# A block's high part meets both parts of x in one product of 512 columns; a tile's two sums share a PSUM bank

## The chip, the cores and the metric

The kernel runs on one core of a Trainium2 chip. Its time is the device time of one launch in microseconds, median of three runs. TensorE (PE) multiplies, with its weight loads shown as an engine of their own (PEld); VectorE (DVE) and ScalarE (ACT) do the elementwise work and read PSUM; GpSimd (POOL) and SyncE (SP) mostly issue DMAs.

## The reference, cut to what matters

x has 256 tokens of 2048 channels, in float32. Three residual parts follow one another, each with large projections of x:

```
x = x + lru_mlstm_layer(rmsnorm(x, e_norm), ...)   # u = x @ w_in; RG-LRU and mLSTM; y @ w_out
x = x + ssd_layer(rmsnorm(x, o_norm), ...)         # u = x @ w_in; SSD scan; y @ w_out
x = rmsnorm(x, final_norm)
h = rmsnorm_2(x, norm_mix)                         # one projection into S5, GLA, differential attention and gates
x = x + merged(h) @ w_out
x = x + ffn(...)                                   # up, convolution, gated silu, down
out = rmsnorm(x, norm_final)
```

Nearly all the arithmetic is in the products of x (or of an activation) with weight matrices of some 2048 x 8000; they must be near float32's accuracy.

## The kernel before

Channels lie on the partitions, the 256 tokens in the free dimension. Every weight matrix is cut on the host into blocks of 128x128, laid out in the order in which PE takes them: one stream of 8048 blocks in chunks of 8 (512 KB). `ahead` (L248) issues a chunk's DMA on SP up to three chunks early, and splits four blocks at a time, up to five such parts ahead: ACT copies them to a rounded float32r tile `wh` (L242), DVE subtracts it from the original and leaves the rest in `wl` (L243). Each has six buffers, given back as PE is through with them.

Activations are split in the same way into a tile of high parts and one of low parts, each [128, 2, 256]: two tiles of channels side by side (`split`, `split_into`; in `finish` with the next norm's weight). `kx` picks the tile of channels k from the pair.

`prod` (L269) multiplies one block: `h` with x's high part, `h` with its low part, `l` with its high part, three matmuls of 256 columns that add up in one PSUM region (L273, L274, L275). `mm` runs it over the KT blocks of each of two output tiles; the group fills one bank [128, 2, 256] from a pool `pm` of four banks. `mm_late` does the same for an output projection, whose first two pairs are begun before the last row tiles are ready, so that two groups are open at once. The other four banks (`ps`) serve the side work. The first layer opens three groups at once while x arrives (`begun`).

What reads a group is one instruction as a rule: DVE multiplies it with the row of 1/rms into a temporary tile (L559, L571, L626, L836, L907, L1030, L1056, L1573), or adds it to the residual (L474, L654); q, k, v and o are copied by ACT (L591 to L598, groups of 4 blocks per tile); in glu ACT takes the tanh of the second tile and DVE multiplies the first with it (L1082, L1083); for the other branches ACT doubles the group (L1101).

RG-LRU, mLSTM, SSD, S5, GLA and attention are generators; `pump`, called at the end of each `mm`, steps them, so their instructions stand between the groups. The framework takes the whole program, plans every engine's order by priorities in a simulated timeline in which buffers are given out in turn, and writes the waits. So the order on DVE and ACT is a planned one, fixed before the launch, and each of them takes its instructions strictly in that order.

Of the kernel before, what the change touches and what calls it, by code (L numbers as in the profile page):

```python
# [80 lines left out]
# per-channel parameters, as columns of 128 channels: name -> number of columns  # L81
# [15 lines left out]
# shape-only constants: name -> columns  # L97
# [17 lines left out]
def _constants():  # L115
# [6 lines left out]
    for r in range(8):  # L122
        c[r::32, COFF["sel8"] + r] = 1.0  # the sum over the four rows r, 32 + r, 64 + r, 96 + r
# [8 lines left out]
    for h in range(4):  # L132
        # rows q, columns k; the first half is the key tile before q's, the second q's own
# [16 lines left out]
class Builder:  # L150
    def __init__(self, nc, tc, d, dbg, ctx):
# [12 lines left out]
        # weight stream  # L164
# [9 lines left out]
        self.w_pos = 0  # blocks taken  # L174
        self.raw, self.hl = {}, {}

# [12 lines left out]
    def act(self, shape=(P, 2, T), dt=F32, pool=None):  # L189
        """storage of the present stage"""  # L190
# [19 lines left out]
    def psm(self, shape=(P, 2, T)):  # L210
        return self.pm.tile(list(shape), F32, name=self.nm("pm"), tag="pm", bufs=4)
# [14 lines left out]
    def _dma_chunk(self, i):  # L226
        """the first chunk comes in halves"""
# [20 lines left out]
    def ahead(self, part):  # L248
        """loads and splits that the blocks from this part on will need"""
# [19 lines left out]
    def prod(self, o, k, KT, xh, xl):  # L269
# [7 lines left out]
    def mm_late(self, KT, k0, np, xh, xl):  # L277
        """the first pairs of output tiles, in the order that late() gives -> PSUM tiles [128, 2, 256]"""
        p = [self.psm() for _ in range(np)]
        for n, k in late(2 * np, KT, k0, np):  # L280
            self.prod(p[n // 2][:, n % 2, :], k, KT, xh, xl)
# [6 lines left out]
    def mm(self, nt, KT, xh, xl):  # L288
        """nt (1 or 2) output tiles of KT blocks each -> PSUM tile [128, nt, 256]"""
        p = self.psm((P, nt, T))  # L290
        for n in range(nt):
            for k in range(KT):
                self.prod(p[:, n, :], k, KT, xh, xl)
# [18 lines left out]
    def drain(self, gen=None):  # L312
        """run the side work (or one piece of it) to its end"""
# [7 lines left out]
    def split_into(self, h, l, v, scale=None):  # L321
        """h, l: parts of v (times a power of two) that one pass carries each"""
# [29 lines left out]
    def colsum(self, tiles, add=True):  # L352
        """sum over the partitions (and over the tiles) -> PSUM [128 tokens, 2]"""
# [12 lines left out]
    def bcast(self, cols):  # L366
        """cols: [128 tokens, 2] -> PSUM [128, 256], row by row the same"""
# [23 lines left out]
    def log1pexp(self, u, w, n):  # L391
        """u = exp(-|x|) in (0, 1] -> log1p(u), as 2 atanh(u / (2 + u)); w: scratch of u's shape"""
# [12 lines left out]
    def conv(self, u, ws, b, taps, dst):  # L405
        """causal convolution along the tokens of one [128, 256] tile"""
# [6 lines left out]
    def exp_exact(self, x, n):  # L413
        """exp of a [128, n] tile to float32's accuracy"""
# [1318 lines left out]
```

## Time and profile before

| | |
|---|---|
| median of 3 runs | 3123.27 us (3122.21 to 3123.41) |
| profiled execution, span | 3120.4 us |
| PE busy, products | 99%, 26310 |
| weight loads busy | 98%, 26310 |
| DVE busy | 74%, 4693 instructions |
| ACT busy | 56%, 3303 instructions |
| DMA | 178 GB/s mean, 55.2% of 16 engines in the weights' queue |

The span runs from the first to the last instruction of the profiled execution; the page gives no other time of it. An engine's share says how long it had something running. The chain of waits goes back from the last instruction to what released it. In the rows, a name such as pm<-x,wh says that an instruction writes tile pm from x and wh; a row of a timeline begins with its start and duration in us, and may merge several instructions of a kind (xN); in brackets stands how long the engine was idle before it, and what ended that.

### The profile page before, as it was taken

To read this page: it belongs to the slowest core of one execution; us is meant where nothing else is said; L and a number is where in the kernel's file an instruction comes from. 1 tells how busy PE (TensorE), PEld (TensorE's weight loads), DVE (VectorE), ACT (ScalarE), POOL (GpSimd) and SP (SyncE) were. 2 spreads that over 40 slices of the span, in tenths; PEclk is the share of its full clock that TensorE was granted. 3 is DMA by queue.
4 is the path that set the end of the run, shared out by engine and by line. 5 is a ranking of instruction groups with operands and counts; after the bars stand their busy time and mean duration, and the time that the engine had idled before them with its cause. 6 is when DMAs were issued, how large, how long until landed. Compare 5 with 4: busy or idle time off the path is not lost.

```text
span 3120.4 us, 66894 instructions
## 1 busy us (share of the span) xinstructions
PE 3097.5 (99%) x26310; PEld 3048.5 (98%) x26310; DVE 2300.0 (74%) x4693; ACT 1748.8 (56%) x3303; POOL 90.9 (3%) x123
## 2 busy tenths in 40 slices
PE   8999999999999999999999999999999999999998
PEld 8999999999999999999999998999999999999998
DVE  8777766669888876778888786666677776567764
ACT  6666544556666555554555554555555555455554
POOL 1000000010000000120000000000000000000000
PEclk9999999999999999999999999999999999999999
DMA  7555555556555555665454554556556555655564
GB/s 236 178 182 161 176 160 183 183 181 213 183 189 175 166 179 179 193 203 173 152 155 149 164 169 149 163 162 199 185 183 184 183 183 184 188 183 184 183 187 151
DMA packets 153933, 556.30 MB, mean 178 GB/s; under 512 B 17392, under 2 KB 18544, under 8 KB 152592
## 3 DMA queue, kind: packets, MB, share of 16 engines
q1 hardware_dynamic: 148752, 534.89, 55.2%
q0 software_dynamic: 3104, 14.75, 1.3%
q8 instruction: 206, 3.38, 0.4%
q10 hardware_dynamic: 1760, 2.38, 0.2%
q14 instruction: 111, 0.91, 0.1%
HBM read 547.69 MB, written 4.26 MB: 177 GB/s over the span
## 4 chain that ended last, share of the span: by engine, by line
PE 99%; DVE 1%; ACT 0%; DMA 0%; issue 0%; SPq 0%; DVEq 0%
PE pm L273 31%; PE pm L275 31%; PE pm L274 31%; PE ps L997 1%; PE ps L1299 0%; PE ps L1337 0%; PE ps L1458 0%; PE ps L362 0%; PE ps L1284 0%; PE ps L1229 0%; PE ps L791 0%; PE ps L966 0%; PE ps L676 0%; PE ps L675 0%; PE ps L1433 0%; DMA w<-w_first 0%
## 5 line engine op out<-in xcount | busy, mean ns | idle before, releaser
L242 ACT CAST wh<-w 128x512 fp32r<-128x512 f32 (+1 forms) x2013 | 1239.3, 621 | 1233.6 <-PE pm L274 1080.1
L243 DVE TENSOR_TENSOR wl<-w,wh 128x512 fp32r<-128x512 f32 (+1 forms) x2013 | 1390.0, 696 | 652.2 <-ACT wh L242 630.4
L273 PE MATMUL pm<-x,wh 128*128 128x256 f32 x5504 | 1566.1, 285 | 5.9 <-ACT wh L242 5.9
L275 PE MATMUL pm<-x,wl 128*128 128x256 f32 x5504 | 1560.1, 284 | 3.1 <-DVE q L419 3.1
L274 PE MATMUL pm<-x,wh 128*128 128x256 f32 x5504 | 1561.4, 284 | 0.0
L273 PEld LDWEIGHTS pm<-x,wh 128*128 128x128 f32 x5504 | 1057.0, 192 | 14.9 <-issue 8.0
L275 PEld LDWEIGHTS pm<-x,wl 128*128 128x128 f32 x5504 | 1056.8, 192 | 6.7 <-DVE wl L243 3.3
L274 PEld LDWEIGHTS pm<-x,wh 128*128 128x128 f32 x5504 | 1057.4, 192 | 2.2 <-issue 1.9
L273 PE MATMUL pm<-a,wh 128*128 128x256 f32 x1712 | 482.3, 282 | 0.5 <-ACT wh L242 0.5
L275 PE MATMUL pm<-a,wl 128*128 128x256 f32 x1712 | 480.7, 281 | 0.0
L274 PE MATMUL pm<-a,wh 128*128 128x256 f32 x1712 | 480.2, 281 | 0.3 <-DVE a L326 0.3
L273 PEld LDWEIGHTS pm<-a,wh 128*128 128x128 f32 x1712 | 321.9, 188 | 0.9 <-ACT wh L242 0.7
L275 PEld LDWEIGHTS pm<-a,wl 128*128 128x128 f32 x1712 | 322.0, 188 | 0.2
L274 PEld LDWEIGHTS pm<-a,wh 128*128 128x128 f32 x1712 | 321.3, 188 | 0.7 <-DVE a L326 0.5
L273 PE MATMUL pm<-h,wh 128*128 128x256 f32 x576 | 163.6, 284 | 0.6 <-DVE t L1083 0.6
L274 PE MATMUL pm<-h,wh 128*128 128x256 f32 x576 | 162.4, 282 | 0.0
L275 PE MATMUL pm<-h,wl 128*128 128x256 f32 x576 | 162.2, 282 | 0.0
L273 PEld LDWEIGHTS pm<-h,wh 128*128 128x128 f32 x576 | 108.4, 188 | 4.6 <-issue 3.1
L274 PEld LDWEIGHTS pm<-h,wh 128*128 128x128 f32 x576 | 108.5, 188 | 0.8 <-issue 0.8
L275 PEld LDWEIGHTS pm<-h,wl 128*128 128x128 f32 x576 | 108.4, 188 | 0.0
L410 DVE SCALAR_TENSOR_TENSOR a<-t,ocw,a 128x255 f32<-128x255 f32 (+1 forms) x144 | 64.6, 476 | 20.6 <-ACT a L408 20.5
L273 PE MATMUL pm<-b,wh 128*128 128x256 f32 x256 | 72.0, 281 | 0.0
(430 smaller groups left out, 2407.7 us busy)
## 6 DMA issues: line engine op xcount, KB each, us to landing
w<-w_up SPq DMA_DIRECT2D x172, 512.0 KB, 3.6
w<-w_w_in_u SPq DMA_DIRECT2D x114, 512.0 KB, 3.6
w<-w_o_in SPq DMA_DIRECT2D x98, 512.0 KB, 3.8
w<-w_w_in_g SPq DMA_DIRECT2D x96, 512.0 KB, 3.6
w<-w_down SPq DMA_DIRECT2D x86, 512.0 KB, 3.5
w<-w_e_in_z SPq DMA_DIRECT2D x64, 512.0 KB, 3.6
w<-w_e_out SPq DMA_DIRECT2D x64, 512.0 KB, 3.5
w<-w_o_z SPq DMA_DIRECT2D x64, 512.0 KB, 3.6
```

What stands on the lines that cost most here:

```text
L242: nc.scalar.copy(h[:, s], w[:, s])
L243: nc.vector.tensor_tensor(l[:, s], w[:, s], h[:, s].bitcast(F32), op=ALU.subtract)
L273: nc.tensor.matmul(o, h, xh(k), start=k == 0, stop=False)
L274: nc.tensor.matmul(o, h, xl(k), start=False, stop=False)
L275: nc.tensor.matmul(o, l, xh(k), start=False, stop=k == KT - 1)
L410: nc.vector.scalar_tensor_tensor(dst[:, j:], u[:, :T - j], ws[taps - 1 - j], dst[:, j:], op0=ALU.mult, op1=ALU.add)
L997: nc.tensor.matmul(o, xdt[s][:, 64 * ee:64 * ee + 64], r, start=s == 0, stop=s == 1, tile_position=(0, 64 * e))
```

## The change

`prod` becomes two matmuls: x's high and low part of one tile of channels now lie side by side in one tile [128, 2, 256], and the block's high part multiplies all 512 columns at once into a bank with two sums; the block's low part multiplies the 256 high columns and adds to the second sum. A group of two tiles takes two banks, and the pool has two such groups in place of four of one bank. Whoever reads a group first adds the two sums (`total`: ACT copies the second, DVE adds the first). q, k, v and o keep the three products of before (`mm_short`). Activations are split by single tiles of channels. In the first layer the third open group takes two banks of the side work's pool. The rest of the diff removes comments and renames pairs of lists.

```
-    def psm(self, shape=(P, 2, T)):
-        return self.pm.tile(list(shape), F32, name=self.nm("pm"), tag="pm", bufs=4)
+    def psm(self, shape=(P, 2, 2, T)):
+        return self.pm.tile(list(shape), F32, name=self.nm("pm"), tag="pm", bufs=2)
...
-        nc.tensor.matmul(o, h, xh(k), start=k == 0, stop=False)
-        nc.tensor.matmul(o, h, xl(k), start=False, stop=False)
-        nc.tensor.matmul(o, l, xh(k), start=False, stop=k == KT - 1)
+        x = X(k)
+        nc.tensor.matmul(o, h, x, start=k == 0, stop=False)
+        nc.tensor.matmul(o[:, 1], l, x[:, 0], start=False, stop=k == KT - 1)
+
+    def total(self, p, scale=None):
+        u = self.tmp()
+        if scale is None:
+            self.nc.scalar.copy(u, p[:, :, 1])
+            self.nc.vector.tensor_tensor(u, p[:, :, 0], u, op=ALU.add)
+        else:
+            self.nc.scalar.mul(u, p[:, :, 1], scale)
+            self.nc.vector.scalar_tensor_tensor(u, p[:, :, 0], scale, u, op0=ALU.mult, op1=ALU.add)
+        return u
+
+    def scaled(self, p, row):
+        u = self.total(p)
+        self.nc.vector.tensor_tensor(u, u, self.two(row), op=ALU.mult)
+        return u
+
+    def mm_short(self, KT, X):
+        nc = self.nc
+        p = self.psm((P, 2, T))
+        for n in range(2):
+            for k in range(KT):
+                h, l = self.block()
+                x, o = X(k), p[:, n]
+                nc.tensor.matmul(o, h, x[:, 0], start=k == 0, stop=False)
+                nc.tensor.matmul(o, h, x[:, 1], start=False, stop=False)
+                nc.tensor.matmul(o, l, x[:, 0], start=False, stop=k == KT - 1)
+        self.pump()
+        return p
...
     def split(self, v, scale=None, pool=None):
-        h, l = self.act(v.shape, F32R, pool), self.act(v.shape, F32R, pool)
-        self.split_into(h, l, v, scale)
-        return h, l
+        out = []
+        for n in range(2):
+            x = self.act(dt=F32R, pool=pool)
+            self.split_into(x[:, 0], x[:, 1], v[:, n], scale)
+            out.append(x)
+        return out
...
     def finish(...)
-            nc.vector.tensor_tensor(x, x if old is None else old, p, op=ALU.add)
+            nc.vector.tensor_tensor(x, x if old is None else old, self.total(p), op=ALU.add)
...
-        begun = [self.psm() for _ in range(3)]
+        begun = [self.psm(), self.psm(), [self.pss(), self.pss()]]
...
-                p = self.mm(2, 8, self.kx(ga_h), self.kx(ga_l))
-                th = self.tmp((P, T))
-                nc.scalar.activation(th, p[:, 1], AF.Tanh, scale=0.5)
-                nc.vector.scalar_tensor_tensor(y[:, n], th, 1.0, p[:, 0], op0=ALU.add, op1=ALU.mult)
+                p = self.mm(2, 8, self.kx(ga))
+                u = self.total(p)
+                nc.scalar.activation(u[:, 1], u[:, 1], AF.Tanh, scale=0.5)
+                nc.vector.scalar_tensor_tensor(y[:, n], u[:, 1], 1.0, u[:, 0], op0=ALU.add, op1=ALU.mult)
```

## Rows read from the trace of the kernel before

**Rows 1.** The page: busy us (share of the span) and instructions of each engine.
```profile
PE 3097.5 (99%) x26310; PEld 3048.5 (98%) x26310; DVE 2300.0 (74%) x4693; ACT 1748.8 (56%) x3303; POOL 90.9 (3%) x123
```

**Rows 2.** The page: the chain that ended last, share by engine.
```profile
PE 99%; DVE 1%; ACT 0%; DMA 0%; issue 0%; SPq 0%; DVEq 0%
```

**Rows 3.** Timeline of PE, up projection: start us, duration us, instruction.
```profile
2450.12 0.28 PE L273 MATMUL pm<-x,wh 128*128 128x256 f32 x1
2450.24 0.28 PE L274 MATMUL pm<-x,wh 128*128 128x256 f32 x1
```

**Rows 4.** The page's groups: count | busy us, mean ns | idle before, releaser.
```profile
L243 DVE TENSOR_TENSOR wl<-w,wh 128x512 fp32r<-128x512 f32 (+1 forms) x2013 | 1390.0, 696 | 652.2 <-ACT wh L242 630.4
L273 PE MATMUL pm<-x,wh 128*128 128x256 f32 x5504 | 1566.1, 285 | 5.9 <-ACT wh L242 5.9
...
L273 PE MATMUL pm<-a,wh 128*128 128x256 f32 x1712 | 482.3, 282 | 0.5 <-ACT wh L242 0.5
...
L273 PE MATMUL pm<-h,wh 128*128 128x256 f32 x576 | 163.6, 284 | 0.6 <-DVE t L1083 0.6
...
L273 PE MATMUL pm<-b,wh 128*128 128x256 f32 x256 | 72.0, 281 | 0.0
```

**Rows 5.** Timeline of PE, first products, granted clock 0.5.
```profile
6.45 0.41 PE L275 MATMUL pm<-x,wl 128*128 128x256 f32 x1
6.66 0.41 PE L273 MATMUL pm<-x,wh 128*128 128x256 f32 x1
```

**Rows 6.** Timeline of PE: RG-LRU's plain float32 products, two in a row.
```profile
72.43 0.59 PE L675 MATMUL ps<-t,lw 128*128 128x256 f32 x2
72.86 0.59 PE L676 MATMUL ps<-t,lw 128*128 128x256 f32 x2
```

**Rows 7.** Timeline of PE: S5's products of 64 columns, merged.
```profile
1531.34 1.84 PE L1299 MATMUL ps<-s5ux,s5bt 128*128 128x64 f32 x15
```

**Rows 8.** Windows: stretch, us; PE, PEld, DVE, ACT, POOL busy (count); clock; DMA.
```profile
682.00:1000.00 318.00, 318.00 (x2658) 307.93 (x2660) 277.04 (x591) 210.82 (x472) 4.83 (x9) 1.00 0.59 189
...
1380.00:1768.00 388.00, 388.00 (x3771) 376.25 (x3771) 326.52 (x1023) 211.71 (x471) 3.13 (x5) 1.00 0.51 159
1768.00:2137.00 369.00, 368.41 (x3047) 352.84 (x3046) 259.55 (x512) 191.79 (x371) 2.51 (x7) 1.00 0.53 162
...
1834.00:1865.00 31.00, 30.41 (x257) 30.20 (x256) 29.01 (x51) 18.26 (x34) 0.31 (x1) 1.00 0.59 178
...
2621.00:2746.00 125.00, 125.00 (x1064) 125.00 (x1063) 68.78 (x105) 56.78 (x93) 0.00 (x0) 1.00 0.60 187
```

**Rows 9.** Timeline, second head's q, k, v, o: group's end, its reader.
```profile
124.51 0.29 PE L275 MATMUL pm<-a,wl 128*128 128x256 f32 x1
...
128.96 0.59 ACT L596 COPY a<-pm 128x512 f32<-128x512 f32 x1
```

**Rows 10.** Timeline of DVE, up projection: the reader of a group.
```profile
2390.99 0.69 DVE L1573 TENSOR_TENSOR t<-pm,r 128x512 f32<-128x512 f32 x1 [0.24 <-PE pm L275]
```

**Rows 11.** Groups by form: the low part of 256 and of 512 elements.
```profile
L326 DVE TENSOR_TENSOR a<-t,a 128x256 fp32r<-128x256 f32 x43 | 18.0, 419 | 0.0
...
L326 DVE TENSOR_TENSOR a<-t,a 128x512 fp32r<-128x512 f32 x24 | 16.4, 683 | 0.4
```

**Rows 12.** Timeline, glu: a group's last products, its reader, who waited.
```profile
1834.23 0.40 PE L275 MATMUL pm<-h,wl 128*128 128x256 f32 x2
...
1857.28 0.41 DVE L1083 SCALAR_TENSOR_TENSOR t<-t,pm 128x256 f32<-128x256 f32 x1
...
1857.75 0.39 PE L273 MATMUL pm<-h,wh 128*128 128x256 f32 x1 [0.59 <-DVE t L1083]
```

**Rows 13.** PE after its longest wait (timeline), and that window's row.
```profile
21.57 0.58 PE L275 MATMUL pm<-x,wl 128*128 128x256 f32 x1 [3.08 <-DVE q L419]
...
21.44:24.85 3.41, 3.28 (x15) 3.28 (x16) 3.41 (x13) 0.45 (x1) 0.00 (x0) 0.50 0.36 113
```

More of the change, by code (lines that the diff above doesn't have):

```diff
@@ L556, in lru @@
             nc.sync.dma_start(lw, d["lru_w"][i].rearrange("p (a b) -> p a b", a=2))
-            p = begun[2] if i == 0 else self.mm(2, 16, XH, XL)
-            u = self.tmp()
-            nc.vector.tensor_tensor(u, p, self.two(rstd), op=ALU.mult)
+            if i == 0:
+                u = self.tmp()
+                for n, p in enumerate(begun[2]):
+                    nc.scalar.copy(u[:, n], p[:, 1])
+                    nc.vector.tensor_tensor(u[:, n], p[:, 0], u[:, n], op=ALU.add)
+                nc.vector.tensor_tensor(u, u, self.two(rstd), op=ALU.mult)
+            else:
+                u = self.scaled(self.mm(2, 16, X), rstd)
             self.add(self.rglru(i, u, lw, sp, hb, yl))
@@ L565, in conv_m @@
         def conv_m(hd):
-            xmh, xml, xch, xcl = [], [], [], []
+            xm_, xc_ = [], []
             for i in range(2 * hd, 2 * hd + 2):
-                p = begun[i] if i < 2 else self.mm(2, 16, XH, XL)
-                u = self.tmp()
-                nc.vector.tensor_tensor(u, p, self.two(rstd), op=ALU.mult)
-                h, l = self.split(u)
-                xmh.append(h)
-                xml.append(l)
+                p = begun[i] if i < 2 else self.mm(2, 16, X)
+                u = self.scaled(p, rstd)
+                xm_ += self.split(u)
                 c = self.tmp()
@@ L630, in layer_one, with out, partial @@
                 nc.vector.tensor_tensor(z, z, (ym if half else yl)[i], op=ALU.mult)
[L631 to L633 removed]
+                ys += self.split(z, 0.5 if half else None)
             if half == 0:
                 self.res = self.load_res(self.x_pair, nc.gpsimd)
[L636 removed]
+                self.partial(ys, 16, LATE["e_out"])
             else:
                 self.acc = []
[L639 to L640 removed]
+                for i, p in enumerate(self.out(ys, 16, LATE["e_out"])):
+                    self.finish(i, p, lambda c: self.par("o_norm", c), self.xs, self.acc)
         self.close(cm)
         self.dump("x1", self.res)
[L644 to L647 removed]
+    def out(self, ys, KT, late):
+        Y = self.kx(ys)
+        yield from self.mm_late(KT, *late, Y)
         for i in range(late[1], 8):
[L649 to L654 removed]
+            yield self.mm(2, KT, Y)
+    def partial(self, ys, KT, late):
+        for i, p in enumerate(self.out(ys, KT, late)):
+            self.nc.vector.tensor_tensor(self.res[i], self.res[i], self.total(p), op=ALU.add)
     def dump(self, name, tiles):
@@ L850, in layer_two @@
         dt, u, s, q, cs = R(), R(), R(), R(), R()
-        nc.vector.tensor_tensor(dt, p[0:H, 0], rstd[0:H], op=ALU.mult)
+        nc.scalar.copy(dt, p[0:H, 0, 1])
+        nc.vector.tensor_tensor(dt, p[0:H, 0, 0], dt, op=ALU.add)
+        nc.vector.tensor_tensor(dt, dt, rstd[0:H], op=ALU.mult)
         nc.vector.tensor_scalar(dt, dt, self.par("dt_bias")[0:H], None, op0=ALU.add)
@@ L1027, in proj @@
         def proj(nt=2, half=False, x=False):
-            p = self.mm(nt, 16, XH, XL)
+            p = self.mm(nt, 16, X)
             u = self.xact() if x else self.act() if nt == 2 else bp.tile([P, nt, T], F32, name="alr")
-            nc.vector.tensor_tensor(u, p, (rhalf if half else rstd).unsqueeze(1).broadcast_to([P, nt, T]), op=ALU.mult)
+            nc.scalar.copy(u, p[:, :, 1])
+            nc.vector.tensor_tensor(u, p[:, :, 0], u, op=ALU.add)
+            nc.vector.tensor_tensor(u, u, (rhalf if half else rstd).unsqueeze(1).broadcast_to([P, nt, T]), op=ALU.mult)
             return u
         u_ssm = [proj() for _ in range(4)]
-        ga_h, ga_l = [None] * 4, [None] * 4
+        ga = [None] * 8
         self.st, scm = self.open("s5")
-        s5 = self.s5(u_ssm, ga_h, ga_l)
+        s5 = self.s5(u_ssm, ga)
         self.s5_entry = self.add(s5, 3)
@@ L1091, in block_two @@
         self.add(diff, 1)
[L1092 to L1093 removed]
+        mx = []
+        for b, yy in enumerate((gb, gc)):
             for i in range(8):
@@ L1104, in block_two @@
                 if b == 1:
-                    h, l = self.split(merged[i], 0.25)
-                    mh.append(h)
-                    ml.append(l)
+                    mx += self.split(merged[i], 0.25)
             if b == 0:
@@ L1358, in s5, with gla @@
                 V.scalar_tensor_tensor(b, b, 1.0, yp, op0=ALU.add, op1=ALU.mult)
-                zh[m // 2], zl[m // 2] = self.split(b, 0.5, self.branch)
+                zx[m - 1:m + 1] = self.split(b, 0.5, self.branch)
             yield
-    def gla(self, alr, qg, kg, vg, rg, oh, ol):
+    def gla(self, alr, qg, kg, vg, rg, ox):
         nc, d = self.nc, self.d
@@ L1473, in gla @@
                                        op0=ALU.mult, op1=ALU.mult)
-            oh[h], ol[h] = self.xact(F32R), self.xact(F32R)
-            self.split_into(oh[h], ol[h], o)
+            for v in range(2):
+                t = ox[2 * h + v] = self.xact(F32R)
+                self.split_into(t[:, 0], t[:, 1], o[:, v])
             yield
```

178 lines of the change are left out of this document (75 added, 103 removed).

## The prediction

> **What bounds the kernel now.** I read the busy shares first: PE 99%, DVE 74%, ACT 56% of a span of 3120.4 us [rows 1]. A busy PE need not be a limiting one, so the chain of waits came next: 99% of it is PE and all other engines together hardly show [rows 2]. Then the timeline of PE in a plain stretch (the up projection): products of 256 columns start every 0.120 us without a gap [rows 3]. So the time is the number of products times 0.120 us, plus the side work's products; what shortens PE's sequence shortens the kernel until something else is late.
>
> How many there are: the first product of a block runs 5504 + 1712 + 576 + 256 = 8048 times [rows 4], so there are 8048 blocks of three products. q, k, v, o of four heads (192 blocks) keep three products in the new kernel; 7856 blocks change.
>
> **The products.** Before, a changed block takes 3 x 0.120 = 0.360 us. After, it takes one product of 512 columns and one of 256, with two weight loads instead of three, and the same 768 columns.
>
> No product of 512 columns of this type is in the trace. Bounds: at clock 0.5 a product of 256 columns takes 0.213 us [rows 5], which is its columns and nothing else, so at full clock 512 columns cost at least 0.213. At most they cost two of today's, 0.240. I take 0.215: the plain float32 products take two in 0.43 us [rows 6], twice the columns' time, beside a 128x128 weight load like ours, so that load is hidden and 0.002 us is left over. If that holds, the 0.013 us by which 256 columns (0.107) miss 0.120 is not a cost of every product but the weight load, which is longer than a short stream. Products of only 64 columns support it: 15 of them last 1.84 us, the last one 0.28, so they start every 0.112 us, although their columns are a quarter of ours; only the load is alike [rows 7].
>
> The second product stays at 256 columns and the next block's load lies behind it: between 0.107 (columns) and 0.120 us; I take 0.120, its price today. Together 0.335; saved 0.025 (0.0245 before rounding) x 7856 = 192 us. About 1200 blocks of the output projections run at 0.1175 (1064 products in 125 us [rows 8]) and save 0.005 less each: 186 us.
>
> The Trainium skill, "TensorE: Matmul & The Clock Gate", section "Back-to-back issue gap", speaks against the change: the gap of a product is its columns at 2.4 GHz plus 2.5 ns, 109 ns for 256. By that rule a block would go from 327.5 to 325 ns and merging would be worth 2.5 ns x 7856 = 20 us. The trace has 120 where the rule says 109 [rows 3], and the same page's section "LDWEIGHTS" (128 columns take 128 / 1.2 GHz, 107 ns) points to the load. For 512 columns the rule gives 216 ns.
>
> **Reading the sums.** By the program's loops 281 groups of tiles leave PSUM; less the 24 of q, k, v, o, 257 change. Each gets an ACT copy of one sum (0.59 us, as the copy of a PSUM tile in [rows 9]) and a DVE addition (0.69, like the PSUM read in [rows 10]); in 16 of them ACT's work only changes. Splits of 68 pairs become two of 256 columns: DVE 2 x 0.419 - 0.683 = 0.155 us more each [rows 11], ACT similar. DVE gains 257 x 0.69 + 68 x 0.155 = 188 us, ACT some 155. That makes DVE 2488 and ACT 1904 us of about 2990: 83% and 64%, beside PE. So it costs nothing where DVE has room, and the stretches tell where it has not [rows 8]:
> - layer two's input (682 to 1000): PE would need 318 - 784 x 0.0245 = 299 us, DVE 277 + 25 x 0.69 = 294. In its fullest stretch with PE nearly unhindered DVE is busy 29.01 of 31 us, 94%. At 95% the stretch takes 310: 11 lost. Bounds: 0 (DVE packs fully) and 19 (no gain there).
> - projections beside S5 (1380 to 1768): PE 388 - 912 x 0.0245 = 366, DVE 326.5 + 29 x 0.69 = 347; at 95% 365, so even. For bursts I take 5; bounds 0 and 22.
>
> **Half as many PSUM groups in flight.** A group takes two banks, so two are in flight instead of four. PE may begin group g+2 only when g is read: the reader has one group's time (32 blocks, 10.7 us; 16 blocks, 5.4) where it had three. In plain stretches the read ends about 0.7 us after the products [rows 10]; with copy, addition and its queue 1.5 to 3: free. In two places it isn't:
> - the gates with glu and gla (1768 to 2137). The reader of a glu tile ran 23 us behind: its products ended at about 1834.5, DVE read it at 1857.28, and PE already waited 0.59 us for that buffer, the fourth [rows 12]. What DVE did ahead of it was the side work of S5 and gla. Adding, over the 40 groups from 1768 to 2137 (in [rows 12] stands the longest), the lag in excess of the next group's time gives 113 us, the upper bound: every excess paid once. The lower is 0: DVE is busy 259.55 of 369 us [rows 8], and the order is planned anew with two buffers. A lag is paid once per backlog and not per group, and while PE stands no weights are split, which is near half of DVE's work there (0.696 us [rows 4] per 4 blocks, 1.44 us of PE): I take a quarter, 28.
> - q, k, v, o: groups of 8 blocks, 2.9 us. One reader per head ends 4.8 us behind [rows 9], behind ACT's RG-LRU work: 1.9 us over, in three heads, 6 us; bounds 0 and 14 (twice that in each of the heads).
>
> Queued behind the new additions on DVE are the weights' low parts, behind the copies on ACT their high parts; both work up to five parts (6.7 us) ahead of PE, so 0.6 to 1.3 us is covered, except where DVE is full, which is counted above.
>
> **Small things.** The begin waits for x and the weights, so its 96 blocks gain nothing: 2 us of the 186 not got. Where one stage's last tiles are the next one's first operand (eight joins) the chain is 1.3 us longer and the window 0.3 to 0.7 shorter; most have room: 6 us, bounds 0 and 16. Weight chunks are wanted every 2.7 instead of 2.9 us; both end well above their landing time, so 0.
>
> **Sum.** 186 - (11 + 5 + 28 + 6 + 2 + 6) = 186 - 58 = 128. Span 3120.4 - 128 = 2992.4; the median of the runs is 2.9 us above the profiled span, so about 2995 us.
>
> **Rivals.**
> - *Columns cost 0.47 ns wherever they stand (slower).* Then 512 columns cost 0.240, PE saves nothing, and the 56 us of waits and full DVE stay, less what DVE regains because PE is slower (about 14): 3123 + 42 = 3165. It decides from a price of 512 columns of 0.232 us on: there a block saves 0.007 us, 58 us in all, and the costs take them. For it: every product at full clock takes 0.1175 to 0.120. Against: half clock and the float32 products [rows 5, 6]. 8%.
> - *Only a product's small constant is saved.* The 0.002 us left over in [rows 6] are all that a merged product gives back: 16 us, against the same 42 to 58: about 3157. Against: 0.120 in [rows 3], which has 0.013 to give. 2%. This is the outcome of the Trainium skill's issue-gap rule above, with the row's constant.
> - *Every product pays 0.013 us of its own.* 512 columns at 0.227, saved 0.013 x 7856 = 104; 3123 - 104 + 58 = 3077. For it: the constant step of [rows 3]. Against: the float32 products don't pay it. 10%.
> - *Two PSUM groups hold PE at every burst.* The gla stretch pays all 113 us: 3123 - 186 + 143 = 3080. For it: PE waited even with four buffers [rows 12]. Against: a lag is a backlog, paid once. 14%. If such waits pass 3 us, the clock may fall too: after PE stood 3.08 us it ran at 0.5 from 21.44 to 24.85 [rows 13], and each time costs about half of those 3.41 us. The Trainium skill, same page, "A second HAM failure mode: psum-queue depth-cycling", tells of PE idling between groups and losing its clock; so far no wait on PSUM in this trace did that.
> - *The second product falls to the load's 0.112 us.* 8 ns x 7856 = 63 more: 2932. For it: [rows 7]. Against: the third product today has the same neighbours and takes 0.120. 6%.
>
> **Chances.** My forecast 60%, own range 2951 (all costs 20 in place of 58, with 192 saved) to 3037 (costs 100). The whole range takes in the three rivals that are still faster: 2930 to 3095. A measurement of this kernel tells some 0.2% (6 us) from no change. Faster: 0.59 + 0.10 + 0.14 + 0.05 = 0.88; same 0.03; slower 0.09, the first two rivals.
>
> **What would show it.** In the plain up stretch a pair of tiles should take 32 x 0.335 = 10.7 us, against 11.5; products of 512 columns start 0.215 us before the next, those of 256 0.120. DVE should stand near 95% and more from 680 to 980 with PE waiting for weights there; PE should have waits for PSUM readers between 1700 and 2050 of some 28 us and little elsewhere. I am wrong if the 512-column product takes 0.227 or more, or if PE's waits add up to far more than 58 us.

## The result, and the profile after

| | median us | runs | ratio to before (95%) |
|---|---|---|---|
| before | 3123.3 | 3122.2 to 3125.1 | |
| changed | 3167.5 | 3163.8 to 3168.9 | 1.0138 (1.0124 to 1.0153) |

The change makes the kernel 44 us slower; 2995 us and a gain were forecast. The profiled execution has a span of 3165.9 us, 45.5 over that of before. The page of the changed kernel, in the columns of [rows 1 and 2]:

```profile
PE 3075.5 (97%) x18454; PEld 2653.4 (84%) x18454; DVE 2449.7 (77%) x5019; ACT 1874.6 (59%) x3613; POOL 92.1 (3%) x123
...
PE 92%; DVE 3%; ACT 2%; issue 0%; DMA 0%; DVEq 0%; ACTq 0%
```

7856 products and as many weight loads are gone, as counted, and PE's busy time fell by 22 us only. The chain of waits has 8% that isn't PE, where it had 1%. Next the groups by line (L276 is the product of 512 columns, L277 the one of 256, L244 the weights' low parts, L284 the new addition, L292 the multiplication by the row of 1/rms behind it; columns as in [rows 4]):

```profile
L276 PE MATMUL pm<-x,wh 128*128 128x512 f32 x5472 | 1940.7, 398 | 25.0 <-DVE t L284 15.2 <-ACT wh L243 6.6 <-DVE s L412 2.2
L277 PE MATMUL pm<-x,wl 128*128 128x256 f32 x5472 | 1542.5, 282 | 3.5 <-DVE wl L244 3.5
...
L244 DVE TENSOR_TENSOR wl<-w,wh 128x512 fp32r<-128x512 f32 (+1 forms) x2013 | 1394.1, 698 | 580.9 <-ACT wh L243 538.2 <-PE ps L1485 1.5 <-PE ps L398 1.0
L284 DVE TENSOR_TENSOR t<-pm,t 128x512 f32<-128x512 f32 x210 | 143.7, 685 | 13.8 <-ACT t L283 13.3
L292 DVE TENSOR_TENSOR t<-t,r 128x512 f32<-128x512 f32 x138 | 94.7, 686 | 0.2
```

"Mean ns of one" overlaps the next product, so the price of a product is read from the starts. The timeline of PE in the up projection, against [rows 3]:

```profile
2499.74 0.28 PE L277 MATMUL pm<-x,wl 128*128 128x256 f32 x1
2499.86 0.39 PE L276 MATMUL pm<-x,wh 128*128 128x512 f32 x1
2500.09 0.28 PE L277 MATMUL pm<-x,wl 128*128 128x256 f32 x1
2500.20 0.39 PE L276 MATMUL pm<-x,wh 128*128 128x512 f32 x1
2500.43 0.28 PE L277 MATMUL pm<-x,wl 128*128 128x256 f32 x1
```

A product of 512 columns starts 0.23 us before the next one, one of 256 0.115. Over all steps of the trace at the full clock the means are 232.6 and 117.7 ns: 350.3 for a block, against 358.2 of three products before. That is 7.9 ns x 7856 = 62 us, not 186.

PE's waits (us in total, times, longest; before, the same list begins with 6.5, 3.1, 2.0, 1.8 and 0.6 us):

```profile
PE pm L276 <- DVE t L284: 27.6, 10, 5.0
PE ps L996 <- DVE a L874: 8.5, 11, 1.1
PE pm L276 <- ACT wh L243: 7.9, 4, 5.4
PE ps L1364 <- DVE s5x L1159: 4.9, 1, 4.9
```

The first is PE at a PSUM tile that VectorE has not read, the last is PE waiting for the scan of S5. Windows of the changed kernel, in the columns of [rows 8]: three stages, then four stretches of 3.4 us around one wait in the first stage.

```profile
697.40:1028.40 331.00, 319.29 (x1895) 266.09 (x1894) 290.48 (x610) 223.89 (x499) 4.85 (x9) 0.99 0.58 182
...
1406.80:1777.70 370.90, 370.90 (x2687) 317.96 (x2687) 327.37 (x990) 219.32 (x479) 3.15 (x5) 1.00 0.55 166
1777.70:2203.30 425.60, 389.06 (x2332) 324.05 (x2331) 300.05 (x632) 220.07 (x439) 3.21 (x8) 0.95 0.46 141
...
59.40:62.80 3.40, 3.40 (x22) 2.96 (x20) 3.31 (x11) 3.09 (x8) 0.00 (x0) 1.00 0.60 161
62.80:66.20 3.40, 0.24 (x2) 0.00 (x0) 3.06 (x7) 0.98 (x3) 0.00 (x0) 1.00 0.40 147
66.20:69.60 3.40, 1.52 (x5) 1.36 (x6) 2.83 (x6) 2.29 (x7) 0.00 (x0) 0.50 0.47 154
69.60:73.00 3.40, 3.40 (x12) 2.92 (x12) 3.34 (x9) 1.62 (x4) 0.00 (x0) 0.50 0.00 0
```

PE stands from 62.8 while VectorE is busy 3.06 of 3.40 us; then 6.8 us run at granted clock 0.5 (1.2 in place of 2.4 GHz). Such stretches add up to 71.7 us ahead of the end, 3.4 before the change. PE has products running in 60.0 and 3.3 us of them, and 3.40 us hold 12 products there where they hold 22 at the full clock: 45% of 56.7, an estimate of some 26 us. The Trainium skill, "TensorE: Matmul & The Clock Gate", section "A second HAM failure mode: psum-queue depth-cycling", tells of a PE that idles briefly and often between PSUM groups and loses its clock. These rows agree in kind, with single waits of 3 to 5 us.

The stages, from the first weight-stream product of one to that of the next; us before, then the difference to before in the changed kernel and in six experiments below:

| stage | before | changed | three products | two groups | read twice | u, up merged | same, GpSimd | changed, paired |
|---|---|---|---|---|---|---|---|---|
| start, through the first q, k, v, o | 85.8 | +18.6 | +19.2 | +0.6 | +2.7 | +2.0 | +1.9 | +17.7 |
| rest of layer one's input | 192.3 | -0.4 | +2.0 | +2.0 | +0.1 | 0 | 0 | -2.1 |
| z, e_out | 398.3 | -2.6 | -0.1 | 0 | -0.1 | 0 | 0 | -7.0 |
| dt, o_in | 319.5 | +11.5 | +15.4 | +7.7 | -0.1 | 0 | 0 | +12.9 |
| o_z, o_out | 378.3 | +0.1 | +2.1 | 0 | +11.0 | 0 | 0 | -5.6 |
| u, projections (beside S5) | 389.0 | -18.1 | -1.9 | 0 | -1.9 | -16.5 | -8.5 | -18.4 |
| gates, glu, gla | 369.0 | +56.6 | +34.3 | +18.3 | +12.2 | +21.1 | +5.6 | +53.3 |
| diff, w_out | 229.2 | -4.1 | -0.2 | -0.2 | +1.6 | 0 | 0 | -5.7 |
| up, down, up, down, end | 753.7 | -16.2 | +2.0 | 0 | +2.0 | -13.6 | -13.7 | -18.8 |

A row counts all that PE does in its stretch, side work too. In the changed kernel 180 of S5's products have moved from the stage of u to the one behind it: 7 of the 18.1 us are no gain, and 7 of the 56.6 no loss. The row of the start is uncertain by 2 to 4 us: the kernel with u and up merged has the start of before and shows +2.0, as the clock stood at 0.5 for 10.2 us there and for 3.4 before.

### The profile page after: what moved, and what is told of

It is laid out like the page before. It is cut to its first block, busy times and chain, and to the rows that moved or that the text cites. A ratio compares the mean times of both kernels' runs of the same rounds, so it can differ in the third digit from the quotient of the medians.

```text
span 3165.9 us, 51959 instructions
## 1 busy us (share of the span) xinstructions
PE 3075.5 (97%) x18454; PEld 2653.4 (84%) x18454; DVE 2449.7 (77%) x5019; ACT 1874.6 (59%) x3613; POOL 92.1 (3%) x123
## 4 chain that ended last, share of the span: by engine, by line
PE 92%; DVE 3%; ACT 2%; issue 0%; DMA 0%; DVEq 0%; ACTq 0%
PE pm L276 56%; PE pm L277 29%; DVE wl L244 1%; PE ps L1027 1%; PE pm L303 1%; ACT wh L243 1%; PE pm L304 1%; PE pm L305 1%; PE ps L1364 1%; PE ps L1326 0%; PE ps L1485 0%; PE ps L996 0%; PE ps L398 0%; PE ps L1311 0%; DVE t L284 0%
## 5 line engine op out<-in xcount | busy, mean ns | idle before, releaser
L276 PE MATMUL pm<-x,wh 128*128 128x512 f32 x5472 | 1940.7, 398 | 25.0 <-DVE t L284 15.2
L244 DVE TENSOR_TENSOR wl<-w,wh 128x512 fp32r<-128x512 f32 (+1 forms) x2013 | 1394.1, 698 | 580.9 <-ACT wh L243 538.2
L277 PE MATMUL pm<-x,wl 128*128 128x256 f32 x5472 | 1542.5, 282 | 3.5 <-DVE wl L244 3.5
L276 PEld LDWEIGHTS pm<-x,wh 128*128 128x128 f32 x5472 | 1032.3, 189 | 272.4 <-issue 24.1
L277 PEld LDWEIGHTS pm<-x,wl 128*128 128x128 f32 x5472 | 1039.5, 190 | 12.5 <-issue 7.1
L276 PE MATMUL pm<-a,wh 128*128 128x512 f32 x1520 | 541.5, 397 | 4.5 <-DVE t L284 2.2
L277 PE MATMUL pm<-a,wl 128*128 128x256 f32 x1520 | 431.1, 284 | 0.0
L276 PEld LDWEIGHTS pm<-a,wh 128*128 128x128 f32 x1520 | 287.1, 189 | 73.2 <-DVE t L284 2.5
L277 PEld LDWEIGHTS pm<-a,wl 128*128 128x128 f32 x1520 | 287.1, 189 | 0.3 <-DVE wl L244 0.3
L276 PE MATMUL pm<-h,wh 128*128 128x512 f32 x576 | 211.0, 404 | 10.2 <-DVE t L284 10.2
L277 PE MATMUL pm<-h,wl 128*128 128x256 f32 x576 | 165.3, 287 | 0.0
L284 DVE TENSOR_TENSOR t<-pm,t 128x512 f32<-128x512 f32 x210 | 143.7, 685 | 13.8 <-ACT t L283 13.3
L276 PEld LDWEIGHTS pm<-h,wh 128*128 128x128 f32 x576 | 110.9, 193 | 40.5 <-issue 14.1
L283 ACT COPY t<-pm 128x512 f32<-128x512 f32 x210 | 121.8, 580 | 9.3 <-PE pm L277 9.2
L277 PEld LDWEIGHTS pm<-h,wl 128*128 128x128 f32 x576 | 111.0, 193 | 0.9 <-issue 0.8
L292 DVE TENSOR_TENSOR t<-t,r 128x512 f32<-128x512 f32 x138 | 94.7, 686 | 0.2
L276 PE MATMUL pm<-b,wh 128*128 128x512 f32 x256 | 89.9, 393 | 0.0
L277 PE MATMUL pm<-b,wl 128*128 128x256 f32 x256 | 72.4, 283 | 0.0
```

The lines of the kernel that those rows point to most:

```text
L244: nc.vector.tensor_tensor(l[:, s], w[:, s], h[:, s].bitcast(F32), op=ALU.subtract)
L276: nc.tensor.matmul(o, h, x, start=k == 0, stop=False)
L277: nc.tensor.matmul(o[:, 1], l, x[:, 0], start=False, stop=k == KT - 1)
L283: self.nc.scalar.copy(u, p[:, :, 1])
L284: self.nc.vector.tensor_tensor(u, p[:, :, 0], u, op=ALU.add)
L292: self.nc.vector.tensor_tensor(u, u, self.two(row), op=ALU.mult)
```

## Experiments

**What a product costs.** A kernel of products alone, no model. Its core:

```
for i in range(n):
    nc.tensor.matmul(p[i % banks][0:M, 0:N], w[dt][:, j, 0:M], x[dt][:, i % 8, 0:N], ...)
```

> Only products in rows of 64, of one type and width, and blocks of both kinds, alone and beside ACT and DVE; nothing of the model is computed. The step from one product's start to the next. If the weight load sets the pace of 256 columns: 64 to 256 columns 0.112 to 0.120, 320 columns 0.136, 384 0.162, 512 0.215, and 256 columns with weights of 64 columns 0.109. If every product pays 0.013 us of its own: 256 0.120, 320 0.147, 384 0.173, 512 0.227, whatever the weights. If columns cost 0.45 ns each: 256 0.117, 384 0.173, 512 0.230, in a straight line through nearly 0. If other engines' traffic is the cause: alone 0.109 and 0.215, beside ACT and DVE 0.120 and 0.232.

The timeline of PE of that kernel, where equal products are one row with their count (rd and rh: 256 and 512 columns of float32r; rf: 384; half: 256 columns with weights of 64; bh: 512 of bfloat16; merg: 512 and 256 in turn):

```profile
60.61 0.88 PE L44 MATMUL rd<-xr,wr 128*128 128x256 f32 x6
...
78.70 1.03 PE L44 MATMUL rf<-xr,wr 128*128 128x384 f32 x5
...
101.98 1.31 PE L44 MATMUL rh<-xr,wr 128*128 128x512 f32 x5
...
164.78 0.73 PE L44 MATMUL half<-xr,wr 128*64 128x256 f32 x5
...
204.75 1.46 PE L44 MATMUL bh<-xb,wb 128*128 128x512 bf16 x6
...
266.83 0.28 PE L53 MATMUL merg<-xr,wr 128*128 128x256 f32 x1
266.95 0.40 PE L52 MATMUL merg<-xr,wr 128*128 128x512 f32 x1
267.19 0.28 PE L53 MATMUL merg<-xr,wr 128*128 128x256 f32 x1
```

In a row of n equal products the last runs its full time and the others one step each: 6 of 256 give (0.88 - 0.28) / 5 = 0.120 us, 5 of 512 (1.31 - 0.40) / 4 = 0.2275. From the starts the steps are 120.0, 146.7, 173.3 and 226.7 ns for 256, 320, 384 and 512 columns (448 takes 206.7): columns at 2.4 GHz plus 13.3 ns. The same weights for all products (loaded 64 times all the same) or two PSUM banks change nothing (120.0, 226.7); half as wide weights, whose load takes 134 in place of 188 to 192 ns, give 113.3 and 230, one shorter and one longer. So the constant does not follow the load. It goes with the type: bfloat16 takes 109.2 and 216 ns. Plain float32 runs each product in two passes of 215.8 or 429 ns, 2.4 ns over twice the columns' time, which is why [rows 6] misled. The closest pair: 512 columns of float32r, and twice 256 in a pass of plain float32, are both 213.3 ns at 2.4 GHz, behind loads of 188 and 190 ns; they take 226.7 and 215.8. Why float32r costs more is open. The Trainium skill, "TensorE: Matmul & The Clock Gate", section "Back-to-back issue gap", gives the gap of an isolated product as its columns and 2.5 ns. bfloat16 agrees here; plain float32 shares only the constant, and float32r doesn't agree. The rows merg show a second loss: 512 and 256 in turn take 353 ns for a pair where the two alone make 346.7, with or without ScalarE and VectorE at work.

**The change without its merging.** The changed kernel, its block in three products of 256:

```
-        nc.tensor.matmul(o, h, x, start=k == 0, stop=False)
+        nc.tensor.matmul(o[:, 0], h, x[:, 0], start=k == 0, stop=False)
+        nc.tensor.matmul(o[:, 1], h, x[:, 1], start=False, stop=False)
```

> The changed kernel with three products of 256 columns per block again (into the same two sums), all else as it is. If the merged product saves the 0.008 us per block that the traces show (350.3 against 358.2 ns): 3167 + 62 = 3229, some less where waits take it up, 3200 to 3230. If the merged product is worth what I forecast and the waits are worse than they look: 3290 and more. If it saves nothing: 3167.

3194.8 us (3193.6 to 3195.1), ratio 1.0224 (1.0209 to 1.0240), a little under the 3200 to 3230 expected: the layout and the reading cost 71.5 us, and the merged product itself gives 27 of the 62 that PE's steps are shorter.

**The two costs by themselves**, in the kernel before: half the PSUM groups, and a second reading of each (its values unchanged).

```
-        return self.pm.tile(list(shape), F32, name=self.nm("pm"), tag="pm", bufs=4)
+        return self.pm.tile(list(shape), F32, name=self.nm("pm"), tag="pm", bufs=2)
...
-        begun = [self.psm() for _ in range(3)]
+        begun = [self.psm(), self.psm(), self.pss()]
```

> The kernel before with two PSUM groups in flight instead of four (of one bank each, and the third of the first layer's in the side work's pool); three products, one reader. If the smaller number of groups is what costs: PE waits at the begin of layer one (18 us) and from 1768 to 2137 (50 us), 3185 to 3200. If the second reading is what costs: at most 3135.

```
+    def again(self, p):
+        u = self.tmp()
+        self.nc.scalar.copy(u, p)
+        self.nc.vector.tensor_tensor(u, p, u, op=ALU.max)
+        return u
...
-            nc.vector.tensor_tensor(u, p, self.two(rstd), op=ALU.mult)
+            u = self.again(p)
+            nc.vector.tensor_tensor(u, u, self.two(rstd), op=ALU.mult)
```

> The kernel before, four groups, three products, but each of the 257 groups is read by ACT and again by DVE, as in the changed kernel (the larger of two equal values in place of a sum; 257 ACT copies but 16, 257 DVE operations more). If the fuller DVE and the longer reading cost little with four groups: 3125 to 3140, all of it from 682 to 1000 and 1768 to 2137. If they are the cause: 3180 and more.

3151.6 us (1.0088, 1.0071 to 1.0105) and 3151.2 (1.0085, 1.0070 to 1.0100): 28 us each. Both fall between the two outcomes that were expected: neither is the loss alone, and they cost alike.

**Both together, and the third difference.** The second kernel has the activations' splits by single tiles of 256 columns, as the changed one has, and nothing else:

```
-        self.split_into(h, l, v, scale)
+        for n in range(2):
+            self.split_into(h[:, n], l[:, n], v[:, n], scale)
```

> The kernel before with two groups at a time and the second reading together, three products, its own splits. Alone they cost 28.0 and 27.5 us; the changed layout with three products costs 71.5. If what is missing (16 us) comes from the two together (a group given back later, of which there are half as many): 3190 to 3196. If they merely add: 3179. If they overlap: 3160 to 3172.

> The kernel before with the activations' splits by single tiles of 256 columns, as the changed kernel has them: two more instructions for each of 36 or so splits, nothing else. If the missing 16 us come from these: 3135 to 3141. If from the joint effect of the groups and the reading: 3123 to 3127.

3184.7 us (1.0196, 1.0179 to 1.0213) and 3123.4 (1.0000, 0.9991 to 1.0009). The two costs come to 61, five over their sum and under the 3190 of a joint effect. The remaining 10 us to the kernel of three products are in the start (+8.1 there against +19.2). The splits cost nothing by themselves; whether they make those 10 beside the other two, or the two sums in two banks do, no run here tells.

**Merged in some stages only.** In the kernel before, with one bank for each output tile: in the feed-forward's up projections (1376 blocks), then in u and the projections too (912 more). And the changed kernel with such one-bank tiles, given back tile by tile.

```
+    def mmw(self, nt, KT, X):
+        p = []
+        for n in range(nt):
+            p.append(self.psm())          # [128, 2, 256], one bank, four of them
+            for k in range(KT):
+                h, l = self.block()
+                x = X(k)
+                self.nc.tensor.matmul(p[n], h, x, start=k == 0, stop=False)
+                self.nc.tensor.matmul(p[n][:, 1], l, x[:, 0], start=False, stop=k == KT - 1)
```

> The kernel before with the merged product in the feed-forward's up projections alone (1376 blocks; one bank for each output tile, the sums added when read), everything else as before. If a block gains 13 ns there and nothing waits, as the changed kernel's two up stages showed (9.2 and 9.0 us): 3105 us. If the gain needs the idle VectorE of a kernel changed throughout, or the readers hold PE: 3115 or more.

> As the one with the up projections, and the stage of u and the projections too (16 columns of tiles fewer products by a third), everything else as before; the gates still take three products. The changed kernel had 18.1 us less in that stage, the one with three products on the changed layout 1.9 less: 16 to 18 us more gained, 3087 to 3090 us. If S5's side work, which runs beside these projections, meets longer readers: 3095 to 3105.

> The changed kernel with a PSUM tile of one bank for each output tile (four of them) in place of two tiles of two banks: the same banks, the same products, but the first output tile of a pair is read and given back while the second is summed. If the two groups (waits of PE for a group's readers) are half of the loss: the 28 us that two groups alone cost, and the start's 19, come back mostly: 3120 to 3140 us. If the waits come from the longer reading alone, or from the load on ScalarE and VectorE: 3155 to 3170.

Up alone: 3109.7 us (3108.1 to 3110.8), 0.9957 (0.9942 to 0.9971), between its two outcomes. Its two stages gained 9.2 and 4.5 us. They hold the same instructions: by the stage's length a block takes 348.3 ns in the first and 353.3 in the second. Tiles of one bank everywhere: 3162.8 (1.0128, 1.0111 to 1.0145), the second of its outcomes: the earlier release, with its reading in twice as many instructions, comes to 5 us.

With u and the projections: 3112.0 (0.9964, 0.9951 to 0.9977), slower than both its outcomes. This run shows where the gain beside S5 goes: the stage of u is 16.5 us shorter and the one behind it 21.1 longer, though its own blocks, their tiles and readers are those of before. Both stages in the columns of [rows 8], then PE's waits in the second:

```profile
1382.00:1754.00 372.00, 372.00 (x2683) 318.48 (x2683) 328.23 (x1015) 220.93 (x503) 3.13 (x5) 1.00 0.52 165
```
```profile
1754.40:2144.50 390.10, 383.41 (x3227) 365.52 (x3226) 273.17 (x577) 199.58 (x396) 3.08 (x8) 0.98 0.49 154
```
```profile
PE ps L1402 <- DMA t<-gla_wg: 3.4, 1, 3.4
PE pm L273 <- DVE t L1110: 2.8, 1, 2.8
PE ps L1371 <- ACT s5yx L1367: 0.5, 1, 0.5
```

Not all of the 16.5 us is gain. The first stage has 860 side products (products of the side work) in place of 1040; the other 180, S5's last, run in the second, where 356 became 536. They take 7.2 us, and merging saves 9.3. Of the 21.1 us, 7.2 are those products, 6.1 are more waits of PE, and most of the rest is the clock, 0.5 for 13.7 us there. So 9.3 us were gained and 13.9 lost.

What ties the two stages is S5: glu's last two row tiles come from its last outputs. PE takes the twelve blocks of glu that need only the others (from 1785.0), then S5's last products, and then stands, 0.5 us for S5's last copy and 3.4 at GLA's first product. The DMA named there was issued by ACT at 1792.4, behind that copy, and VectorE had glu's last input ready at 1797.4. S5's last step but the final transposes is a copy of s5yx, eight times per run; duration min/median/max, then the start of the first and of the last one. In order: before, merged in u and up, changed.

```profile
L1340 ACT COPY s5yx<-ps x8: 372/372/373, 1485.7 to 1763.4; 128x256 f32<-128x256 f32 x8
```
```profile
L1367 ACT COPY s5yx<-ps x8: 372/372/372, 1488.8 to 1790.8; 128x256 f32<-128x256 f32 x8
```
```profile
L1367 ACT COPY s5yx<-ps x8: 372/373/373, 1513.0 to 1815.1; 128x256 f32<-128x256 f32 x8
```

The first product of u starts at 1379.6, 1381.9 and 1406.8 us. So S5 ends 384 us after it before, and 409 and 408 in the others; in the kernel that only reads twice (1393.2 to 1789.8) 397. PE reached glu 412 us after u before, S5's last copy 28 us ahead of it; merged in u and up it reaches glu after 403 us, 6 us ahead of that copy. Of these 34 us PE's earlier arrival is 9, S5's delay is 25. In the changed kernel PE waits 4.9 us for S5's scan, as listed above, and the clock falls. The same stretch, from u to S5's end, as windows of before, then of the kernel merged in u and up:

```profile
1379.60:1763.80 384.20, 384.20 (x3713) 372.67 (x3713) 324.98 (x1020) 210.65 (x469) 3.13 (x5) 1.00 0.51 159
```
```profile
1381.90:1791.20 409.30, 408.83 (x3065) 353.31 (x3064) 355.37 (x1099) 240.06 (x547) 3.13 (x5) 1.00 0.52 163
```

VectorE has 79 operations and 30 us more to do up to there: 57 additions of 0.417 us for the sums read twice, and 21 or so more low parts of weights, since a faster PE calls for the gates' before S5 is through. It is busy 85% of the one stretch and 87% of the other.

**VectorE relieved.** The multiplication by the row of 1/rms on GpSimd, in the last kernel for u and the projections, in the changed kernel for all groups; and the changed kernel with one-bank tiles, this, and every fourth low part of the weights on GpSimd too:

```
-        self.nc.vector.tensor_tensor(u, u, self.two(row), op=ALU.mult)
+        self.nc.gpsimd.tensor_tensor(u, u, self.two(row), op=ALU.mult)
...
+            (nc.gpsimd if i % 4 == 3 else nc.vector).tensor_tensor(l[:, s], w[:, s], h[:, s].bitcast(F32), ...)
```

> The kernel with merged products in up, u and the projections, but the multiplication of u and the projections by the row of 1/rms on GpSimd in place of VectorE (28 of some 0.69 us, 19 us less for VectorE between the start of u and the gated branch). There S5's side work ended 409 us after the start of u, where it ended 384 us after it before the change, and the 16.5 us gained were given back (21.1) in the stage behind. If VectorE's load sets S5's end: S5 ends near 390 us and 15 to 20 us come back, 3092 to 3098. If S5's own chain of steps or the readers' latency does: no change, 3110 to 3114.

> The changed kernel with every group's multiplication by a row of 1/rms on GpSimd in place of VectorE: VectorE has one operation for each group again, as before the change. If VectorE's load is what most of the loss comes through (start +18.6, dt and o_in +11.5, gates and branches +56.6), 35 to 60 us come back: 3108 to 3132. If two groups of two banks are what holds PE, or the latency of three readers one behind the other: GpSimd's slower operation (0.9 us for 256 columns in accum's rows) makes the chain longer, 3165 to 3185.

> The changed kernel with one-bank tiles, row multiplications on GpSimd, and every fourth part of the weights' low halves split on GpSimd as well (some 490 operations of 0.69 us less for VectorE). If VectorE's load explains most of the loss, the merged product's gain is left nearly whole: 3045 to 3090, under both kernels. If GpSimd's slower splits hold PE, or share a way to SBUF with VectorE: 3130 to 3200.

3107.4 us (0.9946, 0.9931 to 0.9961), 3155.1 (1.0101, 1.0086 to 1.0116) and 3192.3 (1.0219, 1.0204 to 1.0234). In the first S5's last copy starts 399 us after u (1780.7 - 1381.8), not near 390. The two stages together are 2.9 us under before, where they were 4.6 over, and the time gains 4.6 of the 15 to 20 us expected: the direction is VectorE's, half of S5's delay and less than a third of the time. The second gives 12 of the 35 to 60 expected. The third came out slower, as its second outcome had it. Its page, then its groups of POOL and DVE:

```profile
PE 3072.2 (96%) x18454; PEld 2650.0 (83%) x18454; DVE 2453.9 (77%) x4603; ACT 1849.1 (58%) x3867; POOL 1044.5 (33%) x793
```
```profile
L247 POOL TENSOR_TENSOR wl<-w,wh 128x512 fp32r<-128x512 f32 x503 | 712.9, 1417 | 1382.7 <-ACT wh L246 1309.1 <-PE pm L280 22.1 <-PE pm L279 11.5
...
L247 DVE TENSOR_TENSOR wl<-w,wh 128x512 fp32r<-128x512 f32 (+1 forms) x1510 | 1185.8, 792 | 548.8 <-ACT wh L246 532.5 <-PE pm L280 7.5 <-PE pm L279 4.1
...
L363 DVE TENSOR_TENSOR a<-t,a 128x256 fp32r<-128x256 f32 x91 | 80.1, 900 | 8.5 <-ACT a L362 4.8
```

VectorE runs 670 operations fewer than with one-bank tiles alone (4603 against 5273) and is busy 2453.9 us where it was busy 2466.4: its weight splits take 792 ns, 698 in the changed kernel, and splits of 256 elements 900, where the changed kernel has 420 for the same group. In this trace the 1059 weight splits on VectorE that no GpSimd instruction overlaps take 686 ns on the mean, the 451 that one overlaps 1041. What runs on GpSimd slows what runs on VectorE beside it, so this is no test of a freer VectorE. That the other two gain less than expected fits it (weight splits take 726 ns in the second).

**The order of lengths.** Products alone again, long and short ones in turn, by twos, fours, eights:

```
+        mix("one", 96, [0, 1])
+        mix("two", 96, [0, 0, 1, 1])
+        mix("eight", 96, [0] * 8 + [1] * 8)
```

> Products alone, no model. In the run of products alone a pair of a 512- and a 256-column product took 353 ns where the two by themselves make 347. If a change of length costs (about 3 ns each way), the pair takes 353 in turn, 350 with two of each kind at a time, and 347.5 with eight of each. If it is the return to the same PSUM bank's second half, the two in different banks take 347 and the order of lengths changes nothing. If it is the place in the stream, none of these changes anything and 512 with 128 or 384 columns is also some 6 ns over the sum of its parts.

In turn 353.4 ns a pair, in two banks too; by twos 348.4, by fours 350.8, by eights 349.1. Length and order do it, not the bank. No rule came out: 512 with 384 takes 413.3 (13.3 over the sum), 384 with 256 is at its sum (293.4), and 512 with 128 takes 340.0, as if the short one cost 113. Timelines, the pairs by twos and the pairs with 128 columns:

```profile
49.65 0.63 PE L73 MATMUL two<-xr,wr 128*128 128x512 f32 x2
50.12 0.39 PE L76 MATMUL two<-xr,wr 128*128 128x256 f32 x2
50.35 0.63 PE L73 MATMUL two<-xr,wr 128*128 128x512 f32 x2
...
131.57 0.44 PE L73 MATMUL m<-xr,wr 128*128 128x512 f32 x1
131.85 0.22 PE L76 MATMUL m<-xr,wr 128*128 128x128 f32 x1
131.91 0.44 PE L73 MATMUL m<-xr,wr 128*128 128x512 f32 x1
```

**By twos in the model**: merged in up alone; in the changed kernel outside the late sums (those of `mm_late`); and merged in up and both layers' z.

```
+            for k in range(0, KT, 2):
+                b = [self.block(), self.block()]
+                for e in range(2):
+                    self.nc.tensor.matmul(p[n], b[e][0], X(k + e), start=k + e == 0, stop=False)
+                for e in range(2):
+                    self.nc.tensor.matmul(p[n][:, 1], b[e][1], X(k + e)[:, 0], start=False, stop=k + e == KT - 1)
```

> The kernel with merged products in up alone, blocks taken two at a time: two products of 512, then two of 256. In the run of products alone that took 348.4 ns for a block where alternating took 353.4; in the up stages alternating took 346.7 ns in one and 353.3 in the other. If the order brings both to 348.4 or less: the second up is 3 us shorter and the first 1 longer, 3107. If the two patterns have another cause: 3110 as before, or 3114 if it makes both 353.

> The changed kernel with blocks taken two at a time outside the late sums (two products of 512, then two of 256): in up alone that gave 348 ns a block in both stages. The stages with a free VectorE should stand at 348 where they stand at 353 (z, o_z: some 3 us in all), and the stretch from u to the gated branches should not move by more than 2 us if VectorE's work sets its end, nor the start: 3160 to 3167. If PE's own steps set the time of every stage, 5 ns less for some 5900 blocks: 3138.

> The kernel before with merged products, two blocks at a time, in up, and in layer one's z and layer two's z as well (1024 blocks more at 360 ns), one bank for each output tile; the rest as before. If those stages have VectorE to spare for the second reading, 12 ns a block: 3106.6 less 12, 3094 to 3097. If the first half of each, beside the mLSTM's and the group norms' side work, gives it back: 3100 to 3105. If the side work is late by more than the products gain: over 3107.

Up alone: 3106.6 us (0.9943, 0.9927 to 0.9960), 350 and 348 ns a block by the stages' length, -8.1 and -7.8 us, as expected. The changed kernel: 3152.5 (1.0090, 1.0075 to 1.0105), 15 us less, more than the 7 that VectorE's theory allowed and half of the 29 that 5 ns for 5900 blocks make. z, o_z, up and down took theirs; u to gla moved by 3.6 us together, since S5's last copy still starts 408 us after u (1395.3 to 1803.4):

```profile
L1372 ACT COPY s5yx<-ps x8: 372/373/375, 1501.0 to 1803.4; 128x256 f32<-128x256 f32 x8
```

Merged in up and both z: **3102.6 us** (3101.7 to 3104.2), 0.9932 (0.9917 to 0.9947), the best of all, 21 us under the kernel before. z, e_out gained 5.8 and o_z, o_out 5.1 us; the start lost 4.6, the rest of layer one's input 1.5, so it missed its 3094 to 3097. It lies in the 3100 to 3105 of the second outcome, though the two z kept 11 of their 12 us.

## Why the prediction was wrong

- **The failed step is the price of the 512-column product.** "If that holds, the 0.013 us by which 256 columns (0.107) miss 0.120 is not a cost of every product but the weight load." It doesn't hold: float32r products of 256, 320, 384 and 512 columns all pay 13.3 ns, the same weights or not. The step was read from plain float32 products [rows 6], another type, and from products at half the clock [rows 5]. The latter was read rightly: at granted clock 0.5 the changed kernel's products of 256 and 512 columns take 213 and 427 ns, their columns alone. But then the half clock shows nothing of a constant that the full clock has. A floor near 113 ns exists at the full clock (192 columns take 109 to 117; [rows 7] has 112), but 256 columns stand above it. Term: 0.2155 (0.215 rounded) forecast, 0.2267 alone, 0.2326 in the kernel.
- **A loss that no step had:** a 512- and a 256-column product in turn take 6.7 ns more than alone. Rival three (every product pays 0.013) was right on the constant; with it alone 104 us would have been saved. Measured it is 62, with the pair's loss and with the output projections, which stood at 353 to 356 ns before and are little better now. They are 1968 blocks, not 1200, which alone is 4 of the 186 us.
- **The second product** was taken at 0.120 and measured 0.1177: right.
- **Waits: 58 forecast, 107 came** (3120.4 - 62 + 107 = 3165.9). PE stands 90.4 us of the span where it stood 22.9, which is 67 of them; the clock is some 26; the remaining 14 stand in no row.
  - q, k, v, o (6, bounds 0 and 14): 14 came, 11 of them in the first head, which takes 28.3 us in place of 17.3 (in the row of the start); PE waits 3.6 and 1.9 us there for readers on ACT (L628, L632).
  - The start (2) lost 18.6 with these 11; ahead of them PE waits 5.0 us at a PSUM tile and 3.5 for a low part of the weights. [Rows 8] could not show it, as no window was put there.
  - Layer two's input (11) was low: the stage is 11.5 us *longer*, after some 6 of gain. The mechanism was another, too: VectorE is busy 290.5 of 331 us, 88% and not 95%, and PE waits for SSD's side work (L996, L899: 11.3 us) and not for weights.
  - The projections beside S5 (5, bounds 0 and 22) were looked at in the wrong stage: their products are 10.8 us shorter, and S5 made PE wait after them.
  - Gates, glu and gla (28) was the largest miss, +56.6, of which 7 are S5's products moved in; two groups alone make 18.3 and the reading alone 12.2.
- **The clock** stood in a rival only, as half of 3.41 us for each long wait [rows 13].
- **Rival one** (columns cost 0.47 ns, 3165) named the time and the point from which it turns, 0.232 for the 512 columns. That its 3165 is so near is a coincidence: 320, 384 and 512 columns follow 0.417 ns and a constant, and its 56 us of waits were 107. The forecast's own test ("I am wrong if the 512-column product takes 0.227 or more, or if PE's waits add up to far more than 58 us") came true on both counts.
- **Rival four** (two groups hold PE at every burst) was right in kind and too high in size for the groups alone: 28 us in a kernel whose PE is slower.

What is shown: the product's price; 28 us for each of the two costs, 61 together; that the gain beside S5 is given back behind it, with S5 late by the same amount in three kernels (408 to 409 us). What is inferred: that VectorE's load sets S5's pace. S5 ended later with each thing added to VectorE (384, 397, 409) and earlier with one taken off (399), but VectorE is busy only 87% there, and the stronger relief slowed it. A rival stands: each of these kernels has an order of its own, planned anew on every engine, and no run holds that order fixed.

## What to carry to other kernels

Before merging products, time the merged form by itself, in its own data type and in the mix in which it will stand: a constant per product read from another type or another clock is not that product's constant. A busy PE at 99% does not mean that shortening PE shortens a stage: look for the side work that must end with it, and how early it ends now. Here 28 us of lead went, 25 of them because the side work itself came later. Apply such a change where the other engines have room (up, z), and leave it out where they don't.

## What had not been expected of the hardware

- A float32r product of 256 to 512 columns costs 13.3 ns beyond its columns at 2.4 GHz (448: 20), bfloat16 2.5 (256 columns: 120.0 and 109.2); a pass of plain float32 takes 215.8 and 429 ns for 256 and 512 columns, 0.833 ns a column and 2.5.
- Products of unlike lengths in turn can cost more than their sum: 512 and 256 353.4 against 346.7 ns, 512 and 384 413.3 against 400.0; by twos 512 and 256 take 348.4. The same instructions ran at 348 or at 353 ns a block in different stages of one execution; why is open.
- A VectorE split of 512 elements took 1041 ns where a GpSimd instruction overlapped it and 686 where none did, in one kernel; the splits of 256 elements took 900 on the mean there, 420 where GpSimd did little.
